# The first layer's input projection by seven products for eight

## The chip, the cores and the metric

One Trainium2 chip, of which the kernel uses one core. The metric is the device time of one execution in microseconds, as the median of the runs shown. A change of some 2% can be told from no change.

## The reference, cut to what matters

Two layers work on 512 latent and 256 context tokens of 2048 features. Each layer norms and modulates its input, projects it with `w_in` to three kinds of heads (HGRN2, mLSTM, attention), and projects the heads' outputs back with `w_out`.

```python
for layer in range(DEPTH):                       # 2
    mod_lat = (silu(c) @ w_mod[layer] + b_mod[layer])[:, None, :]
    mod_ctx = (silu(c_ctx) @ w_mod[layer] + b_mod[layer])[None, None, :]
    shift_l, scale_l, gate_l = jnp.split(mod_lat, 3, axis=-1)
    ...
    pl = split_proj(modulate(x, g_pre[layer], shift_l, scale_l) @ w_in[layer])
    pc = split_proj(modulate(h_ctx, g_pre[layer], shift_c, scale_c) @ w_in[layer])
    a_c, a_l = hgrn2_branch(pc, pl, ...)         # 4 heads
    b_c, b_l = mlstm_branch(pc, pl, ...)         # 4 heads
    c_c, c_l = attention_branch(pc, pl, ...)     # 8 query heads, 2 key heads
    y_lat = jnp.concatenate([a_l, b_l, c_l], axis=-1) @ w_out[layer]
    x = x + gate_l * rms_norm(y_lat, g_post[layer])
    ...
```

`modulate` is `rms_norm(h, gain) * (1 + scale) + shift`.

## The kernel before, in words

Features stand on the partitions, 16 tiles (`kt`) of 128; tokens stand in the columns. Every operand of the projection is a high and a low part in fp32r (`xs[o][kt]`, o = 0 the 512 latent columns, o = 1 two shift columns and the 256 context columns), and so is every weight: `load_w` (L303) loads a quarter of a feature tile's weights (256 KB, `raw`), copies the high part on ScalarE (L309) and subtracts it on VectorE (L310). A product then is three matmuls, high by high, high by low and low by high (L347). One output feature tile of the projection (`Proj`, `run_proj` L366) takes four quarters of four `kt`, each 3 x (512 + 258) columns. There are 61 such tiles in a layer: 20 for attention (`cq`, `ck`, `cv`, `cz`), one for the mLSTM's gates (`bg`, two matmuls for three), 20 for HGRN2 (`aq`, `af`, `ab`, `ai`, `ag`) and 20 for mLSTM (`bq`, `bk`, `bv`, `bo`, `bz`).

The norm's factor of each token (`rb`) is not part of the operand: it multiplies the finished product when VectorE takes it out of PSUM (`evac_`, L586). The shift goes through the projection in two columns of its own and is added as a bias behind it.

The order of the first layer: `emit_start` (L411) computes the modulation's scale on PE (`emit_mod`, L202) while it splits the rows and already multiplies the first six tiles (`EARLY`), whose shift follows by products of its own (L514). The modulation's shift comes by `emit_mods` (L232), and its gate by the same function beside the heads. Then `unit_c` (eight attention heads), `b_gates`, four times `unit_a` and four times `unit_b` run; each head calls `proj` for each of its tiles just before it needs it. `add_mod` (L248) meanwhile sums the next layer's shift and scale on VectorE, one row of weights at a time (L255, L257). The heads' results go to memory (`mixd`), one of them directly into an operand (`DIRECT`, L396), and `project_mid` (L1139) multiplies them with `w_out`. The second layer then does the same with its own weights.

A scheduler orders each engine's instructions ahead of time; what stands in a `high_priority` context goes first. Every DMA is issued from SP's queue in order. The heads' tiles have mostly one buffer each (`U`, `PAIR`), `raw`, `hi` and `lo` four, the staging tiles `st` seven. PSUM has eight banks: `psP` two times two, `psW` two, `psS` two.

## Time and profile before

| | us |
|---|---|
| median of 2 runs | 2874.87 (2874.21 to 2875.53) |
| span of the profiled execution | 2873.6 |
| PE busy | 2846.9 |
| PE weight loads busy | 2515.7 |
| DVE busy | 1867.5 |
| ACT busy | 1134.7 |
| POOL busy | 17.1 |

The span goes from the first to the last instruction of one profiled execution; the runs' times include what lies around it. PE is TensorE, DVE VectorE, ACT ScalarE, POOL GpSimd, SP the engine whose queue issues the DMAs. Matmul records overlap, so the pace of PE is read from how many matmuls a stretch holds and not from the mean of one record.

### The profile page before, as it was taken

The numbers are of one execution on the slowest core, as the hardware profiler recorded it, in microseconds if no ns is written. First come the engines' busy times: TensorE is split into PE (matmuls) and PEld (weight loads), VectorE is DVE, ScalarE is ACT, GpSimd is POOL, SyncE is SP. The second block draws the span as 40 slices with busy tenths as digits, with TensorE's granted clock in tenths as the row PEclk, the third lists the DMA queues.
The fourth block names the chain that finished last, engine by engine and source line by source line (L and its number), as shares of the span: only waits on it lengthen the run. The fifth ranks groups of instructions, "written<-read, shape, count | busy, mean of one in ns | idle before, by whom it ended". The sixth has DMA issues, their size and how long they took to land.

```text
span 2873.6 us, 51559 instructions
## 1 busy us (share of the span) xinstructions
PE 2846.9 (99%) x19849; PEld 2515.7 (88%) x19849; DVE 1867.5 (65%) x4203; ACT 1134.7 (39%) x2475; POOL 17.1 (1%) x32
## 2 busy tenths in 40 slices
PE   9999999999999999999999999999999999999998
PEld 4648878988888888888999999999899999999886
DVE  3405547667657868688768879567667665757526
ACT  3203423344433432332656654444533333333433
POOL 0000000000000000000000000000000000000000
PEclk9999999999999999999999999999999999999999
DMA  9564355322222325353667765224222222424545
GB/s 333 173 194 140 107 173 160 92 87 56 58 61 71 99 86 151 107 157 114 199 195 214 231 178 169 63 79 132 74 67 64 67 70 81 139 82 138 158 128 158
DMA packets 208280, 366.76 MB, mean 128 GB/s; under 512 B 24704, under 2 KB 42384, under 8 KB 207904
## 3 DMA queue, kind: packets, MB, share of 16 engines
q1 hardware_dynamic: 208032, 363.45, 42.1%
q8 instruction: 156, 2.56, 0.4%
q14 instruction: 92, 0.75, 0.1%
HBM read 345.08 MB, written 18.28 MB: 126 GB/s over the span
## 4 chain that ended last, share of the span: by engine, by line
PE 95%; ACT 2%; DVE 1%; DMA 1%; issue 1%; SPq 0%; DVEq 0%; ACTq 0%
PE pp L347 72%; PE pp L1329 6%; PE ops L1075 2%; PE modps L232 2%; PE scps L1035 2%; PE lv L788 2%; PE ptps L1068 1%; PE modps L202 1%; PE aops L869 1%; PE modp L263 1%; PE tps L626 1%; PE sps L851 1%; PE nps L962 1%; PE cps L942 1%; PE nps L960 1%
## 5 line engine op out<-in xcount | busy, mean ns | idle before, releaser
L347 PE MATMUL pp<-x0h,hi 128*128 128x256 f32 (+2 forms) x3088 | 942.1, 335 | 3.8 <-ACT x0h L398 2.3
L347 PE MATMUL pp<-x0l,hi 128*128 128x256 f32 (+2 forms) x3088 | 934.4, 332 | 0.0
L347 PE MATMUL pp<-x0h,lo 128*128 128x256 f32 (+1 forms) x3056 | 921.3, 332 | 0.0
L309 ACT CAST hi<-raw 128x512 fp32r<-128x512 f32 x764 | 472.3, 620 | 1084.3 <-PE pp L347 828.9
L310 DVE TENSOR_TENSOR lo<-raw,hi 128x512 fp32r<-128x512 f32 x764 | 526.2, 691 | 429.9 <-ACT hi L309 393.0
L347 PEld LDWEIGHTS pp<-x0h,hi 128*128 128x128 f32 x3088 | 544.6, 189 | 77.6 <-issue 15.3
L347 PEld LDWEIGHTS pp<-x0l,hi 128*128 128x128 f32 x3088 | 543.4, 189 | 66.7 <-issue 12.8
L347 PEld LDWEIGHTS pp<-x0h,lo 128*128 128x128 f32 x3056 | 536.5, 188 | 61.1 <-issue 9.2
L347 PE MATMUL pp<-x1h,hi 128*128 128x258 f32 (+1 forms) x1632 | 463.6, 285 | 0.3 <-ACT hi L309 0.3
L347 PE MATMUL pp<-x1l,hi 128*128 128x258 f32 (+1 forms) x1632 | 463.8, 284 | 0.0
L347 PE MATMUL pp<-x1h,lo 128*128 128x258 f32 (+1 forms) x1600 | 454.0, 284 | 0.4 <-DVE lo L310 0.2
L347 PEld LDWEIGHTS pp<-x1h,hi 128*128 128x128 f32 x1632 | 310.7, 190 | 14.0 <-issue 11.9
L347 PEld LDWEIGHTS pp<-x1l,hi 128*128 128x128 f32 x1632 | 308.6, 189 | 7.2 <-issue 6.9
L347 PEld LDWEIGHTS pp<-x1h,lo 128*128 128x128 f32 x1600 | 302.9, 189 | 5.6 <-issue 4.4
L257 DVE SCALAR_TENSOR_TENSOR scs<-st,sc,scs 128x512 f32<-128x512 f32 x180 | 135.4, 752 | 1.5 <-DMA st<-in_wmod 1.4
L257 DVE SCALAR_TENSOR_TENSOR mo<-st,sc,mo 128x512 f32<-128x512 f32 x180 | 135.4, 752 | 0.0
L1329 PE MATMUL pp<-lo,x0h 128*128 128x512 f32 x256 | 101.5, 396 | 0.0
L1329 PE MATMUL pp<-hi,x0h 128*128 128x512 f32 x256 | 101.3, 396 | 0.0
L1329 PE MATMUL pp<-hi,x0l 128*128 128x512 f32 x256 | 100.4, 394 | 0.0
L802 ACT COPY lvc<-aqq 128x256 f32<-128x256 f32 x140 | 60.4, 431 | 95.8 <-DVE aqq L810 74.7
L1069 ACT COPY pt<-ptps 128x512 f32<-128x512 f32 x96 | 47.5, 516 | 113.5 <-PE ptps L1068 113.0
L807 DVE TENSOR_TENSOR akk<-akk,aff 128x256 f32<-128x256 f32 x168 | 76.2, 453 | 9.3 <-PE ktps L835 7.0
(383 smaller groups left out, 3092.8 us busy)
## 6 DMA issues: line engine op xcount, KB each, us to landing
raw<-in_win SPq DMA_DIRECT2D x500, 256.0 KB, 2.7
st<-in_wmod SPq DMA_DIRECT2D x325, 256.0 KB, 2.9
raw<-in_wout SPq DMA_DIRECT2D x192, 256.0 KB, 3.2
raw<-in_wlast SPq DMA_DIRECT2D x80, 256.0 KB, 2.8
mw<-in_wmod SPq DMA_DIRECT2D x57, 256.0 KB, 5.3
st<-in_win SPq DMA_DIRECT2D x24, 256.0 KB, 3.9
xr<-in_xin SPq DMA_DIRECT2D x48, 128.0 KB, 3.5
st<-mixd SPq DMA_DIRECT2D x45, 128.0 KB, 3.6
```

Source lines behind the costliest of these rows:

```text
L232: prev = T.matmul(ps[32 * j:32 * j + 32, :], scs[:, 32 * kt:32 * kt + 32], ws[j], start=(i == 0 and (side or g == 0)), stop=(i == 1 and (s ...
L257: V.scalar_tensor_tensor(out=acc, in0=w, scalar=c, in1=acc, op0=ALU.mult, op1=ALU.add)
L309: S.copy(out=hi, in_=raw)
L310: lo_ins[:] = [V.tensor_tensor(out=lo, in0=raw, in1=hi.bitcast(F32), op=ALU.subtract).ins]
L347: T.matmul(dst, self.w[w][:, kt % 4, :], xs[o][kt][j][:, x0:x0 + n], start=(first and i == 0 and (self.outs is None or self.outs[k][1])), ...
L788: prev = T.matmul(lv[64 * c:64 * c + 64, o:o + 64], km[:, t0:t0 + 64], qm[:, t1:t1 + 64], start=True, stop=True, tile_position=(0, 64 * c) ...
L802: S.copy(out=mixed(qm.unsqueeze(1), 0, 256, b, 0), in_=mixed(Q2, c0, 256, b))
L807: V.tensor_tensor(out=x, in0=x, in1=blocks(F2, c0, b, b, 776, True), op=ALU.mult)
L1035: T.matmul(x[:, d0:d0 + len_], q[:, a, COLP[c]:COLP[c] + P], kr[:, b, k0:k0 + len_], start=(i == 0), stop=(i == 2))
L1069: S.copy(out=pt[:, 0:len(g) * P], in_=tp)
L1075: T.matmul(o[:, i * P:i * P + P], vt[kb], pt, start=(k == 0), stop=(k == len(mine) - 1))
L1329: x = T.matmul(ps[c], xs[0][kt][a][:, c * P:c * P + P], w[b].rearrange("p a b -> p (a b)"), start=(kt == kts[0] and i == 0), stop=(kt == k ...
```

## The change: what it does

The first layer's projection is no longer done tile by tile. The rows (2048 input features) are taken in two halves of eight `kt`. Within a half, a pair of output tiles (two 128-wide feature tiles), two groups of four `kt` and two halves of the tokens (256 latent, 2 shift and 128 context columns each, `BW` = 386) make a 2 x 2 by 2 x 2 block product. It is done with seven products for eight, with sums of blocks of the weights (`s1` to `s4`, on GpSimd) and of the rows (`T1`, `T2`, `T3`, `N4`, made once for each half). Accumulators in four PSUM banks (W, X, Y, Z) are copied out between products (`snap`) and added up (`end`). `bg` has no partner and takes four products of two matmuls.

The first half is done for all 31 units (`PAIRS`) in `emit_start`, before any head; partial sums go to memory (`pd`). The second half (`emit_second`) is done in the heads' phase, a pair when one of its tiles is first asked for; it loads the partial sums, adds to them (snapshots on GpSimd, ends on VectorE) and stores the finished products to memory (`qd`). A head then loads its product with three DMAs (`fetch`), and GpSimd multiplies it by `rb`.

The early tiles and their shift products are gone. Four chunks of the modulation come first (scale 4, 5 and shift 0, 1, of the first half's features); twelve others, the gate and the next layer's shift among them, are multiplied on PE beside the first half's products, and the next layer's scale is summed on VectorE there, so that none of it is left beside the heads. In the first layer there are four staging buffers, six for `raw` and three for `hi` and `lo`. The operands of `project_mid` and the second layer get their place after the first layer's heads.

```diff
+CSEQ = [n for g in range(2) for n in [f"ck{g}", f"cv{g}"] + [f"{p}{h}" for h in range(4 * g, 4 * g + 4) for p in ("cq", "cz")]]
+ASEQ = [f"{p}{h}" for h in range(4) for p in ("aq", "af", "ab", "ai", "ag")]
+BSEQ = [f"{p}{h}" for h in range(4) for p in ("bq", "bk", "bv", "bo", "bz")]
+PAIRS = [tuple(q[i:i + 2]) for q in (CSEQ, ["bg"], ASEQ, BSEQ) for i in range(0, len(q), 2)]
...
+    class Pool:
+        st, raw, hl, stp = 4, 6, 3, None
+        def tile(self, *a, **k):
+            return self.pool.tile(*a, **k)
+    wp, psP = Pool(), Pool()
...
+    pd, qd = ({n: tc.dram_tile([P, 2, BW], F32, name=f"{c}_{n}") for u in PAIRS for n in u} for c in ("pd", "qd"))
...
+    def emit_mod(l, n):
         ps = sps(512, "modps")
-        for kt in range(KT):
-            if kt == 8 and between is not None:
-                between()
-            if kt < len(slots):
-                w = slots[kt]()
-                nc.sync.dma_start(w, I["wmod"][l, n, kt])
-            else:
-                w = stage(I["wmod"][l, n, kt])
-            j = kt % 4
-            T.matmul(ps[32 * j:32 * j + 32, :], scs[:, 32 * kt:32 * kt + 32], w,
-                     start=(kt < 4), stop=(kt >= 12), tile_position=(0, 32 * j))
+        for g in range(4):
+            ws = [stage(I["wmod"][l, n, 4 * g + j]) for j in range(4)]
+            prev = None
+            for j in (3, 2, 1, 0):
+                kt = 4 * g + j
+                with tc.issue_after(prev) if prev is not None else nullcontext():
+                    prev = T.matmul(ps[32 * j:32 * j + 32, :], scs[:, 32 * kt:32 * kt + 32], ws[j],
+                                    start=(g == 0), stop=(g == 3), tile_position=(0, 32 * j)).ins
+            if g < 3:
+                yield
...
+    B11, B21, T2, T1, T3, B22, N4 = [(g, i) for g in range(4) for i in range(2)][0:7]
+    XB = {}
...
+    def squares(sc, b, first):
+        if first:
+            acc[0] = sc.tile([P, 2, BW], F32, name="acc")
+            S.activation(out=acc[0], in_=b, func=AF.Square)
+        else:
+            sq = sc.tile([P, 2, BW], F32, tag="sq", name="sq")
+            S.activation(out=sq, in_=b, func=AF.Square)
+            G.tensor_tensor(out=acc[0], in0=acc[0], in1=sq, op=ALU.add)
...
+    def sum_blocks(sc, j, b1, b2, E):
+        t1, t2 = (sc.tile([P, BW], F32, tag=f"t{i}{j}", name=f"t{i}{j}") for i in range(2))
+        E.tensor_tensor(out=t1, in0=b1[:, 1], in1=b1[:, 0], op=ALU.subtract)
+        E.tensor_tensor(out=t2, in0=b2[:, 1], in1=t1, op=ALU.subtract)
+        E.tensor_tensor(out=b1[:, 1], in0=b2[:, 1], in1=b1[:, 1], op=ALU.subtract)
+        return t1, t2
...
+    def split_blocks(bs, E):
+        for blk in (B11, B21, T2, T1, T3, B22, N4):
+            g, i = blk
+            for j, (b1, b2, t1, t2) in enumerate(bs):
+                src = {B11: b1[:, 0], B21: b2[:, 0], T2: t2, T1: t1, T3: b1[:, 1], B22: b2[:, 1], N4: t2}[blk]
+                if blk == N4:
+                    E.tensor_tensor(out=t2, in0=b2[:, 0], in1=t2, op=ALU.subtract)
+                if i == 0:
+                    XB[g, j] = [wp.tile([P, 2 - (g == 3), BW], F32R, tag=f"X{g}{j}{c}", name=f"X{g}{c}") for c in "hl"]
+                h, lo = (x[:, i] for x in XB[g, j])
+                S.copy(out=h, in_=src)
+                V.tensor_tensor(out=lo, in0=src, in1=h.bitcast(F32), op=ALU.subtract)
...
+    def split_w(src):
+        hi, lo = (wp.tile([P, 4, P], F32R, tag=c, name=c, bufs=wp.hl) for c in ("hi", "lo"))
+        S.copy(out=hi, in_=src)
+        V.tensor_tensor(out=lo, in0=src, in1=hi.bitcast(F32), op=ALU.subtract)
+        return hi, lo
...
+    def add_w(a, b, op, tag=None):
+        o = wp.tile([P, 4, P], F32, tag=tag, name=tag, bufs=1) if tag else b
+        G.tensor_tensor(out=o, in0=a, in1=b, op=op)
+        return o
+    def product(ps, w, blk, first, parts=((0, 0), (0, 1), (1, 0))):
+        g, i = blk
+        for j in range(4):
+            for k, (a, b) in enumerate(parts):
+                T.matmul(ps[:, 0:BW], w[a][:, j, :], XB[g, j][b][:, i], start=(first and j == 0 and k == 0),
+                         stop=(j == 3 and k == len(parts) - 1), skip_group_check=not first)
...
+    def two_tiles(l, unit, half, psx, snap, end):
+        bank = lambda t: psx.tile([P, 512], F32, tag=t, name=f"ps{t}")
+        src = lambda f, k: raw_w(I["win"][l, TIDX[unit[f]], 2 * half + k])
...
+        with urgent():
+            a11, a12, a21, a22 = src(0, 0), src(0, 1), src(1, 0), src(1, 1)
+            w = split_w(a11)
+        X = bank("X")
+        product(X, w, B11, True)
+        snap(0, 0, X)
+        with urgent():
+            w = split_w(a12)
+            s1 = add_w(a21, a22, ALU.add, "s1")
+            s2 = add_w(s1, a11, ALU.subtract, "s2")
+        W = bank("W")
+        product(W, w, B21, True)
+        end(0, 0, W)
+        with urgent():
+            w = split_w(s2)
+        product(X, w, T2, False)
+        snap(0, 1, X)
+        with urgent():
+            w = split_w(s1)
+            s3 = add_w(a11, a21, ALU.subtract)
+        Y = bank("Y")
+        product(Y, w, T1, True)
+        snap(1, 1, Y)
+        with urgent():
+            w = split_w(s3)
+            s4 = add_w(a12, s2, ALU.subtract)
+        product(X, w, T3, False)
+        snap(1, 0, X)
+        end(1, 1, X)
+        with urgent():
+            w = split_w(s4)
+        product(Y, w, B22, False)
+        end(0, 1, Y)
+        with urgent():
+            w = split_w(a22)
+        Z = bank("Z")
+        product(Z, w, N4, True)
+        end(1, 0, Z)
...
+        g = emit_mod(0, 4)
+        next(g)
+        early_consts()
+        list(g)
+        list(emit_mod(0, 5))
+        bs = []
+        for j in range(4):
+            b = raw_blocks(sc, j, j)
+            for i, x in enumerate(b):
+                squares(sc, x, i == j == 0)
+                scale_blocks(0, x, j + 4 * i)
+            bs.append((*b, *sum_blocks(sc, j, *b, V)))
+        split_blocks(bs, V)
+        for n in (0, 1):
+            list(emit_mod(0, n))
+        put_shifts(sc)
+        late_consts()
...
+        adds = [(1, 4 + j, kt) for j in range(4) for kt in range(KT)]
+        for u, unit in enumerate(PAIRS):
+            pt = [wp.tile([P, 2, BW], F32, tag="pt", name="pt", bufs=3) for _ in unit]
+            def snap(f, h, ps, sign=1):
+                with tc.high_priority():
+                    S.activation(out=pt[f][:, h], in_=ps[:, 0:BW], func=AF.Copy, scale=float(sign))
+            def end(f, h, ps, n=len(unit)):
+                with tc.high_priority():
+                    if n == 1 and h == 0:
+                        S.copy(out=pt[f][:, h], in_=ps[:, 0:BW])
+                    else:
+                        V.tensor_tensor(out=pt[f][:, h], in0=ps[:, 0:BW], in1=pt[f][:, h], op=ALU.add)
+                    if (f, h) in ((0, 1), (1, 0)):
+                        nc.sync.dma_start(pd[unit[f]], pt[f])
+            two_tiles(0, unit, 0, psx, snap, end)
+            prio[0] = True
+            for _ in range(2):
+                mod_step()
+            for _ in range(2 + u % 2):
+                if adds:
+                    add_mod(*adds.pop(0), accs=accs)
+            if u >= 21 and u - 21 < 4:
+                j = u - 21
+                if j == 0:
+                    bs = []
+                b = raw_blocks(sc, j, 8 + j)
+                for i, x in enumerate(b):
+                    kt = 8 + j + 4 * i
+                    squares(sc, x, False)
+                    scale_blocks(0, x, kt)
+                    G.tensor_copy(x[:, 0, 256:258], modt[0][:, kt, :])
+                bs.append((*b, *sum_blocks(sc, j, *b, G)))
+        while adds:
+            add_mod(*adds.pop(0), accs=accs)
+        split_blocks(bs, G)
+        cols = [acc[0][:, h, c:c + P] for h in range(2) for c in (0, P)] + [acc[0][:, h, 258:BW] for h in range(2)]
+        token_rstd(const, cols, 6, rb, (0, CO), "rs")
...
+    def emit_second(psx):
+        def second_half(unit):
+            pt = []
+            with urgent():
+                for nm in unit:
+                    pt.append(wp.tile([P, 2, BW], F32, tag="pt", name="pt", bufs=3))
+                    nc.sync.dma_start(pt[-1], pd[nm])
+            def snap(f, h, ps, sign=1):
+                with tc.high_priority():
+                    t = wp.tile([P, BW], F32, tag="sn", name="sn", bufs=4)
+                    S.activation(out=t, in_=ps[:, 0:BW], func=AF.Copy, scale=float(sign))
+                    G.tensor_tensor(out=pt[f][:, h], in0=pt[f][:, h], in1=t, op=ALU.add)
+            def end(f, h, ps):
+                with tc.high_priority():
+                    V.tensor_tensor(out=pt[f][:, h], in0=ps[:, 0:BW], in1=pt[f][:, h], op=ALU.add)
+                    if (f, h) in ((0, 1), (1, 0)):
+                        nc.sync.dma_start(qd[unit[f]], pt[f])
+            two_tiles(0, unit, 1, psx, snap, end)
+            made.update(unit)
+        return second_half
...
+                while nm not in made:
+                    second_half(units.pop(0))
...
+        def fetch(nm, dst):
+            nc.sync.dma_start(dst[:, 0:NL].rearrange("p (h c) -> p h c", h=2), qd[nm][:, :, 0:256])
+            nc.sync.dma_start(dst[:, NL:NL + 130], qd[nm][:, 0, 256:BW])
+            nc.sync.dma_start(dst[:, NL + 130:XW], qd[nm][:, 1, 258:BW])
...
+                fetch(nm, dst)
+                G.tensor_tensor(out=dst[:, 0:XW], in0=dst[:, 0:XW], in1=rb, op=ALU.mult)
...
+    units, made = list(PAIRS), set()
+    with tc.tile_pool(name="ws", bufs=1) as ws, \
+            tc.tile_pool(name="psX", bufs=1, space=bass.MemoryType.PSUM) as psx:
+        wp.pool = ws
+        with tc.tile_pool(name="first", bufs=1) as sc:
+            wp.stp = sc
+            emit_start(sc, psx)
+        second_half = emit_second(psx)
+        emit_lb()
+        with tc.tile_pool(name="unit0", bufs=1, reuse_waits="tile") as up:
+            run_units(0, False, up, [])
+    wp.st, wp.raw, wp.hl, wp.stp = 7, 4, 4, None
+    xp = ctx.enter_context(tc.tile_pool(name="xp", bufs=1, reuse_waits="tile"))
+    for kt in range(KT):
+        if kt != DIRECT:
+            new_x(kt, xp)
+    wp.pool = ctx.enter_context(tc.tile_pool(name="wp", bufs=1, reuse_waits="tile"))
+    psP.pool = ctx.enter_context(tc.tile_pool(name="psP", bufs=2, space=bass.MemoryType.PSUM, reuse_waits="tile"))
+    with tc.tile_pool(name="post0", bufs=1, reuse_waits="tile") as pp:
```

## Rows read from the trace of the kernel before

**Rows 1.** The page, part 1: engine, busy us (share of the span), instructions.
```profile
PE 2846.9 (99%) x19849; PEld 2515.7 (88%) x19849; DVE 1867.5 (65%) x4203; ACT 1134.7 (39%) x2475; POOL 17.1 (1%) x32
```

**Rows 2.** Stretches: us, busy of PE, PEld, DVE, ACT, POOL (instructions), clock, DMA share, GB/s.
```profile
0.00:230.00 230.00, 222.48 (x1019) 119.66 (x1020) 68.25 (x170) 49.98 (x84) 0.20 (x4) 0.99 0.69 229
230.00:626.00 396.00, 394.99 (x2621) 340.48 (x2620) 240.45 (x497) 144.20 (x288) 1.48 (x2) 1.00 0.42 129
626.00:1020.00 394.00, 392.14 (x2929) 343.96 (x2929) 277.04 (x680) 163.78 (x413) 0.21 (x1) 1.00 0.24 68
726.26:826.51 100.25, 100.25 (x750) 88.13 (x750) 64.07 (x162) 39.35 (x102) 0.00 (x0) 1.00 0.21 57
1020.00:1419.00 399.00, 399.00 (x2548) 360.11 (x2547) 308.63 (x657) 140.25 (x334) 8.62 (x15) 1.00 0.45 131
```

**Rows 3.** The chain of waits: start, us, what.
```profile
925.89 30.91 PE pp L347 x176
...
1500.05 83.40 PE pp L347 x708
...
2692.28 36.62 PE pp L1329 x158
```

**Rows 4.** PE, 230 to 1419 us, groups by shape: count | busy us, mean ns.
```profile
L347 PE MATMUL pp<-x0h,hi 128*128 128x512 f32 x874 | 349.4, 400 | 0.3 <-DVE aqq L586 0.3
...
L1075 PE MATMUL ops<-pt,lvc 128*128 128x128 f32 x352 | 44.3, 275 | 0.0
L1035 PE MATMUL scps<-ckr,cqr 128*128 128x256 f32 x192 | 28.6, 286 | 0.0
...
L1068 PE MATMUL ptps<-c_ident,pr 128*128 128x128 f32 x176 | 25.8, 274 | 0.0
...
L232 PE MATMUL modps<-st,scs 128*32 128x512 f32 x128 | 17.0, 605 | 0.0
```

**Rows 5.** DVE, 230 to 1419 us, groups by line.
```profile
L310 DVE TENSOR_TENSOR lo<-raw,hi 128x512 fp32r<-128x512 f32 x231 | 159.8, 692 | 124.8 <-ACT hi L309 117.9 <-PE tps L626 4.5 <-DMA raw<-in_win 1.5
L257 DVE SCALAR_TENSOR_TENSOR scs<-st,sc,scs 128x512 f32<-128x512 f32 x120 | 90.4, 753 | 1.5 <-DMA st<-in_wmod 1.4
...
L807 DVE TENSOR_TENSOR akk<-akk,aff 128x256 f32<-128x256 f32 x84 | 38.3, 456 | 1.6 <-ACT aff L756 0.3
...
L586 DVE TENSOR_TENSOR zb<-pp,rb 128x770 f32<-128x770 f32 x8 | 7.7, 965 | 1.3 <-PE lv L788 1.3
```

**Rows 6.** POOL in order of time: start us, us, instruction, idle before.
```profile
1157.61 0.86 POOL L918 TENSOR_SCALAR_AFFINE_SELECT dexp<-dexp 128x768 f32<-128x768 f32 x1 [43.98 <-DVE mo L257]
...
1345.59 0.86 POOL L918 TENSOR_SCALAR_AFFINE_SELECT dexp<-dexp 128x768 f32<-128x768 f32 x1 [43.75 <-DVE scs L257]
1347.86 1.13 POOL L918 TENSOR_SCALAR_AFFINE_SELECT dexp<-dexp 128x768 f32<-128x768 f32 x1 [1.41 <-ACT dexp L915]
...
2486.13 0.63 POOL L918 TENSOR_SCALAR_AFFINE_SELECT dexp<-dexp 128x512 f32<-128x512 f32 x1 [72.26 <-ACT dexp L915]
```

**Rows 7.** DVE in order of time, at two of those moments.
```profile
1158.03 0.98 DVE L310 TENSOR_TENSOR lo<-raw,hi 128x512 fp32r<-128x512 f32 x1 [0.50 <-ACT hi L309]
...
1345.38 0.96 DVE L586 TENSOR_TENSOR zv<-pp,rb 128x770 f32<-128x770 f32 x1
```

**Rows 8.** DMA: loads, KB, us to landing; and the first 72 us.
```profile
st<-in_wmod SPq DMA_DIRECT2D x325, 256.0 KB, 2.9
...
DMA packets 13828, 23.96 MB, mean 333 GB/s; under 512 B 2816, under 2 KB 3200, under 8 KB 13824
```

**Rows 9.** All engines in order of time, at the start and at the heads' end.
```profile
19.82 1.05 PE L207 MATMUL modp<-c_sel,mo 128*128 128x2 f32 x8 [0.79 <-DVE mo L204]
...
217.53 0.69 DVE L238 COPY mo<-modps 128x512 f32<-128x512 f32 x1 [7.26 <-PE modps L232]
...
221.43 0.39 PE L347 MATMUL pp<-x1h,hi 128*128 128x258 f32 x1
...
1404.66 0.69 DVE L396 TENSOR_TENSOR x0l<-mix,x0h 128x512 fp32r<-128x512 f32 x1
```

More of the change, by code (lines that the diff above doesn't have):

```diff
@@ L22 @@
 XW = NL + 2 + NC
+BW = 386
 CO = NL + 2
@@ new lines, in emit, with scale_blocks @@
+    acc = [None]
+    def squares(sc, b, first):
[6 more added lines that the diff above has]
+            G.tensor_tensor(out=acc[0], in0=acc[0], in1=sq, op=ALU.add)
+    def scale_blocks(l, b, kt):
+        for v, c in enumerate((slice(0, 256), slice(258, BW))):
+            S.activation(out=b[:, :, c], in_=b[:, :, c], func=AF.Copy, scale=gs[l][:, kt, v:v + 1])
```

330 lines of the change are left out of this document (134 added, 196 removed).

## Prediction

> **What bounds the kernel now.** I read the page's busy shares first [rows 1]: TensorE (PE) is busy 99% of the span and VectorE (DVE) 65%. That PE share alone proves little, because matmul records overlap, so I went to the chain of waits [rows 3]: long runs of matmuls with nothing between them. 176 projection matmuls, alternately 512 and 258 columns wide, take 30.91 us: 351 ns per pair. 708 of 256 columns take 83.40 us (117.8 ns each), 158 of 512 columns 36.62 us (231.8 ns). PE is paced by columns and is the bound from about 23 us on. The table of stretches [rows 2] then says what stands next to it: between 230 and 1419 us DVE works 240.45 + 277.04 + 308.63 = 826 us of 1189, so it has 30% left; GpSimd (POOL) does almost nothing. One HGRN2 head takes 100.25 us: five tiles of 16 x 3 x 0.351 = 16.85 us make 84.2, so 16.0 us are the head's own PE work, and DVE is busy 64.07 us beside it. The first layer's heads end when the last mixed head is split, at 1406 us [rows 9]. What follows is the same code before and after but for pools, 2873.6 - 1406 = 1467 us.
>
> **The change, part by part.** The sum is made against the profiled span; the median of the runs lies 1.3 us above it, which I add at the end.
>
> *Products.* 386 columns lie between two measured widths: 117.8 + 130 x (231.8 - 117.8)/256 = 175.7 ns. One of the seven products of half a pair has 4 x 3 matmuls, 2.11 us; a pair's half takes 7 x 2.11 = 14.75 us, against 2 x 16.85 / 2 = 16.85 before. Thirty pairs, both halves: 60 x (16.85 - 14.75) = 126 us less for PE. The gates' tile has no partner and costs the same 11.2 us as before.
>
> *Start.* Before, the first product runs at 23 us, while the modulation still arrives, and the first 230 us hold only six tiles (101 us of products). After, nothing is multiplied until four chunks of the modulation (scale 4 and 5, shift 0 and 1) are in, since a product needs scaled, summed and split rows with their shift columns. Loads run through four staging buffers, and the four matmuls of a group are queued behind the load issued last. So a group costs its landing, 2.9 us for one load, about 0.7 us for each of three more (256 KB at the 333 GB/s of the first 72 us would be 0.79) [rows 8], and 1.06 us of matmuls (17.0 us for 16 groups [rows 4]): 6.0 us. 16 groups: 96 us. Add 4 us to the first load and the last chunk's way to the first product, 3.9 us from copy to matmul [rows 9], with the shift columns 6: first product at 106 us. Bounds: 85 if transfers overlap better, 125 if landings are as slow as when everything loads at once. The splitting of the rows lies under those loads.
>
> *First half of the rows.* 30 x 14.75 + 5.6 = 448 us of products. Twelve further chunks of modulation stand on PE beside them: 48 x 1.06 + 12 x 1.05 for their sums over partitions [rows 9] = 64 us; four chunks on DVE end in matmuls, 6 us. Together 518 us. Per pair (17.3 us of PE) DVE has seven splits, four additions and 2.5 modulation rows of two 0.75 us operations: 4.8 + 2.2 + 3.8 = 10.8 us, so PE stays the bound. The staging ring is tight: 10.5 loads per pair through four buffers of some 6 us a turn are 15.8 us. If it were slower, up to 25 us.
>
> *Between the halves.* The second half's split rows take the tiles of the first. Their order is that of the products, and a block's split (4 x 0.55 us) is as long as a product, so little shows: 8 us, from 3 to 20.
>
> *Second half with the heads.* Products 448 us. The heads' own PE work: in 1177 us up to 1406, 858 full steps (of 874) of 3 x 0.351 us and 16 of the gates are 915 us, output projection 12, gates' modulation 17, sums 15; 218 remain. PE alone would need 448 + 218 = 666 us, where before the same heads were spread over some 1180. This is the point on which the change hangs: DVE's work for the heads is not reduced by as much. Its groups in that stretch [rows 5] (some 120, four of the largest shown) add up to 921 us; 160 are weight splits, 188 modulation, 53 the scaling by the norm, 24 other, and 496 the heads. Records overlap a little (826 busy of 921 added, 0.90), so the heads are 445 us. Each pair adds 7 x 0.62 us of splits and 4 x 0.50 us of additions out of PSUM, 6.3 us. The scaling goes to POOL.
>
> I take this half in two. Attention: PE has ten pairs, 98.7 us of head work in three groups [rows 4] and some 16 in smaller ones, 262 us; DVE has 124 of the heads (138 added, of lines 1007 to 1077 and of the queries' and gates' lines 589 and 600) and 63 of the pairs, 187. PE binds, 262. The rest: PE has 404 us; DVE has 445 - 124 = 321 and 20.5 x 6.3 = 129, 450 us. **DVE binds there**, and with no gap at all.
>
> POOL is the disputed cost. Per pair it gets four additions of 512 columns, four of 386, and two scalings of 770. No row shows a two-input operation on POOL; the nearest are one-input masks, 0.63 us for 512 columns and 0.86 for 768 [rows 6]. By those (low end) a pair costs 4 x 0.63 + 4 x 0.53 + 2 x 0.86 = 6.4 us; if its inputs are read one after the other (high end) 12.8. In the rest that is 130 to 260 us. The rows show that it isn't free to DVE: a split that takes 0.69 us took 0.98 [rows 7] when it began 0.42 us into a mask of 0.86, as long as if it had waited for the mask's end, and a mask begun under a DVE operation took 1.13 instead of 0.86. About three quarters of DVE's time is in operations that read SBUF twice or copy it, like these; those out of PSUM were not lengthened (0.96 us for a scaling [rows 7] with the mask of 1345.59 us beside it, as on average [rows 5]). [...]
>
> I take the low price, nearest in size and engine, and half of it as delay (65 us), since POOL also runs under DVE's PSUM operations and under the heads' waits for PE and ScalarE. Second half: 262 + 450 + 65 = 777 us.
>
> Moving the products through memory costs no engine time of its own. The fetches stand in SP's queue, where one that waits for its tile holds the weight loads behind it; six raw buffers cover about a pair and a half of products, so I price it at nothing, 20 us if that cover is gone. The early shift products (some 8 us on PE) fall away in the start. DMA volume grows by about 60 tiles x four passes of 0.39 MB, 95 MB, at about 43% busy engines in this stretch [rows 2]: hidden.
>
> **The sum.** 106 + 518 + 8 + 777 + 1467 = 2876, and 1.3: 2877 us. The gain of the seventh product is given back because the heads no longer have their products' time to hide DVE in.
>
> **The rivals.**
> (a) PE stays the bound, or DVE without delay: products run ahead and POOL's work falls in gaps. T of the second half 666 to 712, total 2766 to 2812. For it: the order of each engine is free to mix pairs into the heads' waits, and DVE's average use in the second half, (445 + 190)/712, would still be under 90%. Against it: after attention DVE's own work already exceeds PE's.
> [...]
> (c) The change doesn't do what it says: PE stalls inside the first half, on the staging ring or on snapshots that must leave a bank before the next product adds to it. A bank has one product (2.1 us) of grace against about 0.5 us on ScalarE. Ring and start at their upper bounds: 2877 + 19 + 25 = 2921.
>
> **How the numbers follow.** Forecast (2815 to 2932) with (c) 0.44, (a) 0.27, (b) 0.29. Forecast's own range 2815 to 2930. To hold 8 in 10 the range takes in most of both sides: 2775 to 2980. Within 2% (2817 to 2932), about what a measurement can tell from no change, 0.44; faster by more 0.27, slower by more 0.29.
>
> **What would show it.** First product near 106 us; first half about 518 us with matmuls 176 ns apart; then, after attention, DVE above 85% busy and PE with idle stretches that DVE or POOL end. [...] I am wrong if the first half isn't bound by PE, if POOL's two-input price lies outside 0.63 to 1.27 us, or if the mixed heads end well before the products do.

## The result, and the profile after

The changed kernel takes 3214.3 us (3213.6 to 3215.0), against 2874.9 us before: ratio 1.118, 95% interval 1.115 to 1.122. The forecast was 2877 us (2775 to 2980). The kernel is 339 us slower, and no case I had worked out reaches so far.

The first two parts of the page of the changed kernel, to be set beside [rows 1]:

```profile
PE 2792.9 (87%) x19065; PEld 2568.5 (80%) x19065; DVE 2221.5 (69%) x4474; ACT 1360.6 (42%) x2953; POOL 679.1 (21%) x495
...
PE   2599999987899888873337999999999999999998
...
PEclk9999999999999999986668999999999999999999
```

The rows of digits show the span in 40 slices, the busy share of each in tenths. PE, which filled 99% of the span, now has two holes: the first two slices, and three slices of 3 from 1445 us on (18 slices of 80.3 us), in which its granted clock falls too. The table of stretches of the changed kernel shows the same by stage (us, then busy time of PE, PEld, DVE, ACT and POOL, the granted clock, the DMA share and GB/s); its counterpart is [rows 2].

```profile
0.00:138.00 138.00, 40.43 (x169) 10.82 (x169) 39.94 (x111) 38.51 (x68) 32.64 (x24) 1.00 0.59 195
138.00:704.00 566.00, 541.76 (x3126) 484.19 (x3126) 364.30 (x552) 200.19 (x385) 193.34 (x144) 0.99 0.67 216
704.00:1065.00 361.00, 322.08 (x1970) 309.07 (x1971) 292.98 (x474) 182.72 (x379) 200.81 (x140) 0.96 0.45 143
1065.00:1420.00 355.00, 298.35 (x1968) 277.67 (x1966) 325.34 (x544) 169.46 (x393) 186.12 (x136) 0.95 0.40 128
1420.00:1720.00 300.00, 117.50 (x870) 102.36 (x870) 201.17 (x542) 108.97 (x315) 59.33 (x41) 0.68 0.19 58
1720.00:3211.00 1491.00, 1472.77 (x10965) 1384.37 (x10965) 997.79 (x2255) 660.77 (x1417) 6.85 (x10) 0.99 0.42 130
```

Read from the top: 138 us until the first product; 566 us of the first half of the rows, PE almost full; attention beside the second half's products until 1065; HGRN2 heads beside products until 1420, DVE 92% busy; then 300 us in which the heads are alone, PE 39% and DVE 67% busy, so that no engine is full; then the same end as before. DVE's timeline of the changed kernel shows when each mixed head leaves (HGRN2 heads `ag`, mLSTM heads `bz`; two of the latter left out); before, the last left at 1403 us and was split at 1406 [rows 9]:

```profile
1229.46 0.68 DVE L778 TENSOR_TENSOR mix<-mixps,ag 128x512 f32<-128x512 f32 x1
...
1363.47 0.68 DVE L778 TENSOR_TENSOR mix<-mixps,ag 128x512 f32<-128x512 f32 x1
...
1466.12 0.69 DVE L778 TENSOR_TENSOR mix<-mixps,ag 128x512 f32<-128x512 f32 x1 [1.70 <-PE mixps L776]
...
1541.72 0.68 DVE L778 TENSOR_TENSOR mix<-mixps,ag 128x512 f32<-128x512 f32 x1
...
1588.96 0.69 DVE L778 TENSOR_TENSOR mix<-mixps,bz 128x512 f32<-128x512 f32 x1 [1.63 <-PE mixps L776]
...
1717.38 0.69 DVE L778 TENSOR_TENSOR mix<-mixps,bz 128x512 f32<-128x512 f32 x1 [1.63 <-PE mixps L776]
```

While products run beside it, an HGRN2 head takes 134 us (1229 to 1363). Alone it takes 75 us (1466 to 1542), and an mLSTM head alone some 45. The last product is stored at 1426 us, when two HGRN2 heads and all four mLSTM heads are still to be finished: the products have run ahead of the heads.

DVE's groups of the changed kernel, 704 to 1720 us (busy us, mean ns, idle time before); splits were 692 ns before [rows 5]:

```profile
L466 DVE TENSOR_TENSOR lo<-raw,hi 128x512 fp32r<-128x512 f32 x119 | 106.8, 898 | 14.7 <-ACT hi L465 14.5
L466 DVE TENSOR_TENSOR lo<-s,hi 128x512 fp32r<-128x512 f32 x90 | 74.7, 834 | 5.9 <-ACT hi L465 5.5
L961 DVE TENSOR_TENSOR aqq<-aqq,aff 128x256 f32<-128x256 f32 x84 | 59.9, 713 | 0.9 <-ACT lvc L953 0.6 <-DVE lvc L952 0.3
L958 DVE TENSOR_TENSOR akk<-akk,aff 128x256 f32<-128x256 f32 x84 | 52.6, 626 | 1.1 <-ACT aff L907 0.6
...
L952 DVE COPY lvc<-akk 128x256 f32<-128x256 f32 x84 | 35.2, 419 | 0.1
```

POOL's additions by line (ns: least, median, most), all of two inputs: weight sums of 512 columns (one of the four kinds left out), and the second half's additions of 386:

```profile
L480 POOL TENSOR_TENSOR raw<-raw x62: 1263/1413/1899, 33.5 to 1393.7; 128x512 f32<-128x512 f32 x62
L480 POOL TENSOR_TENSOR s<-s,raw x60: 1259/1464/2545, 32.3 to 1395.7; 128x512 f32<-128x512 f32 x60
L480 POOL TENSOR_TENSOR s<-raw,s x60: 1264/1295/2866, 35.4 to 1409.0; 128x512 f32<-128x512 f32 x60
...
L647 POOL TENSOR_TENSOR pt<-pt,sn x121: 858/1068/5412, 704.1 to 1418.6; 128x386 f32<-128x386 f32 x121
```

The least weight sum, 1.26 us, is my high bound for POOL, and the medians (1.29 to 1.46) lie beyond it; I had taken the low one, 0.63, from masks [rows 6].

### The profile page after: what moved, and what is told of

Same layout as the page of the kernel before. It is cut to its first block, busy times and chain, and to the rows that moved or that the text cites. A ratio compares the mean times of both kernels' runs of the same rounds, so it can differ in the third digit from the quotient of the medians.

```text
span 3211.4 us, 52468 instructions
## 1 busy us (share of the span) xinstructions
PE 2792.9 (87%) x19065; PEld 2568.5 (80%) x19065; DVE 2221.5 (69%) x4474; ACT 1360.6 (42%) x2953; POOL 679.1 (21%) x495
## 4 chain that ended last, share of the span: by engine, by line
PE 50%; DVE 9%; issue 3%; DMA 3%; ACT 2%; POOL 1%; SPq 0%; DVEq 0%; POOLq 0%; ACTq 0%
PE pp L324 32%; PE pp L1474 5%; PE psX L487 2%; PE ops L1226 1%; PE lv L939 1%; PE psY L487 1%; DVE lo L466 1%; PE scps L1186 1%; PE psW L487 1%; DVE akk L958 1%; DMA st<-mixd 1%; PE ptps L1219 1%; DVE aqq L961 1%; PE nps L1111 1%; DVE aff L962 1%
## 5 line engine op out<-in xcount | busy, mean ns | idle before, releaser
L324 PE MATMUL pp<-x0h,hi 128*128 128x256 f32 (+1 forms) x2112 | 551.6, 304 | 1.2 <-ACT hi L286 1.1
L324 PE MATMUL pp<-x0l,hi 128*128 128x256 f32 (+1 forms) x2112 | 547.2, 302 | 0.0
L324 PE MATMUL pp<-x0h,lo 128*128 128x256 f32 (+2 forms) x2096 | 540.5, 302 | 0.1
L324 PEld LDWEIGHTS pp<-x0h,hi 128*128 128x128 f32 x2112 | 361.1, 189 | 16.0 <-ACT hi L286 1.6
L324 PEld LDWEIGHTS pp<-x0l,hi 128*128 128x128 f32 x2112 | 361.0, 189 | 15.7
L324 PEld LDWEIGHTS pp<-x0h,lo 128*128 128x128 f32 x2096 | 356.3, 189 | 13.8 <-DVE lo L287 0.5
L324 PE MATMUL pp<-x1h,hi 128*128 128x258 f32 (+1 forms) x656 | 186.6, 285 | 4.7 <-ACT x1h L373 4.1
L324 PE MATMUL pp<-x1l,hi 128*128 128x258 f32 (+1 forms) x656 | 187.5, 286 | 0.3 <-DVE x1l L374 0.3
L324 PE MATMUL pp<-x1h,lo 128*128 128x258 f32 (+1 forms) x640 | 182.2, 286 | 0.8 <-DVE lo L287 0.7
L480 POOL TENSOR_TENSOR s<-raw,s 128x512 f32<-128x512 f32 x60 | 88.0, 1466 | 343.2 <-DVE lo L466 297.6
L324 PEld LDWEIGHTS pp<-x1h,hi 128*128 128x128 f32 x656 | 126.2, 193 | 6.0 <-ACT x1h L373 4.5
```

The lines of the kernel that those rows point to most:

```text
L324: T.matmul(dst, self.w[w][:, kt % 4, :], xs[o][kt][j][:, x0:x0 + n], start=(first and i == 0 and (self.outs is None or self.outs[k][1])), ...
L480: G.tensor_tensor(out=o, in0=a, in1=b, op=op)
```

## The experiments

In what follows "the heads' stretch" is from the end of the first half (703 us, the same in most runs) to the split of the last mixed head; it was 1016 us in the changed kernel. A time without an interval is a single run's, read beside the changed kernel's 3214.3; the runs of one kernel lie up to 13 us apart (3192.9 to 3206.0), so single differences of 5 or 10 us say nothing by themselves.

**Products first.** The edit:

```
+            while units:
+                second_half(units.pop(0))
+            with tc.issue_after(last_end[0]):
+                fetch_(nm, dst)
```

> The computation is whole; only the order changes: no head of the first layer fetches a finished product before the last product of the second half has left its bank. So the second half falls into products alone (P) and heads alone (H), and the time is about 704 + P + H + 1491 us (the stretches before and behind are those of the changed kernel). Theory 'late heads' (the heads are a serial chain that now starts only at 704 us, and the products no longer cover it): P near 455 us (30 pairs of 14.75 us and the gates), since nothing but PE binds products that stand alone, and H 600 to 680 us (four HGRN2 heads of 75 us and four mLSTM heads of 47 us, as the changed kernel's last ones take when alone, and about 130 for attention); total 3250 to 3330. Rival 'POOL's price' (sums of weights and of products on POOL at 1.2 to 1.5 us pace the products themselves): P above 560 us, over 18.5 us per pair, and total above 3350 or H well under 600.

Measured: 3310.5 us. The tie of SP's fetches to DVE's last addition held nothing back: POOL scales the first fetched product at 733 us, and attention went on beside the products. What the run did is to put all products ahead of all heads in the program's order. The last product was stored at 1314 us for 1426, and the last head ended at 1818 for 1719, with HGRN2 heads of 73 us and mLSTM heads of 46, all eight alone. P and H can't be read apart, so the numbers fit by the total only. What follows: products that end 112 us earlier gave nothing; heads that came later ended 99 us later.

**Heads first.**

```
+            prio[0] = False
             two_tiles(0, unit, 1, psx, snap, end)
+            prio[0] = True
```

> The loads, sums and splits of the second half's weights lose their precedence over the heads' instructions; all else is as in the changed kernel. Theory 'late heads' with products that run ahead: products then spread over the heads, the stretch in which heads run alone with PE at 40% (1426 to 1720 us) shrinks, and the time falls to 2950 to 3100 us. [...]

Measured: 3224.4 us, ratio 1.120 (1.119 to 1.122): not the 2950 to 3100 of my theory. The heads' last split is at 1734 us, and again the products are all stored (1436 us) long before. The loads' precedence isn't why products run ahead: the order of the engines lets them run ahead with or without it.

**No POOL.**

```
-                    S.activation(out=t, in_=ps[:, 0:BW], func=AF.Copy, scale=float(sign))
-                    G.tensor_tensor(out=pt[f][:, h], in0=pt[f][:, h], in1=t, op=ALU.add)
+                    V.tensor_tensor(out=pt[f][:, h], in0=pt[f][:, h], in1=ps[:, 0:BW],
+                                    op=ALU.add if sign > 0 else ALU.subtract)
...
-                G.tensor_tensor(out=dst[:, 0:XW], in0=dst[:, 0:XW], in1=rb, op=ALU.mult)
+                V.tensor_tensor(out=dst[:, 0:XW], in0=dst[:, 0:XW], in1=rb, op=ALU.mult)
...
-        G.tensor_tensor(out=o, in0=a, in1=b, op=op)
+        (G if prio2[0] else V).tensor_tensor(out=o, in0=a, in1=b, op=op)
```

> In the second half nothing of the products or of the scaling is left on POOL: the sums of weights and the scaling by the norm run on DVE, and the partial sums are added by DVE straight out of PSUM, without the copy on ScalarE. [...] Theory 'late heads': DVE gets some 6 us more per pair of products (190 us in a stretch of 1016 in which it is busy 830), wins some 80 back by shorter splits, and the time stays between 3170 and 3290, with the heads still alone at the end.

Measured: 3204.4 us, ratio 1.113 (1.110 to 1.115). The stretch from 704 to 1710 us in this run (columns as above), and DVE's groups in it:

```profile
704.00:1710.00 1006.00, 725.90 (x4798) 690.30 (x4796) 802.40 (x1850) 413.92 (x959) 10.48 (x18) 0.86 0.36 113
```

```profile
L467 DVE TENSOR_TENSOR lo<-raw,hi 128x512 fp32r<-128x512 f32 x118 | 81.0, 686 | 1.8 <-ACT hi L466 1.5
...
L648 DVE TENSOR_TENSOR pt<-pt,psX 128x386 f32<-128x386 f32 x91 | 50.3, 553 | 12.3 <-PE psX L488 12.1
L960 DVE TENSOR_TENSOR akk<-akk,aff 128x256 f32<-128x256 f32 x84 | 37.8, 449 | 3.4 <-ACT aff L909 3.1
L963 DVE TENSOR_TENSOR aqq<-aqq,aff 128x256 f32<-128x256 f32 x84 | 37.6, 448 | 1.2 <-ACT lvc L955 1.2
L954 DVE COPY lvc<-akk 128x256 f32<-128x256 f32 x84 | 24.6, 292 | 0.1
...
L481 DVE TENSOR_TENSOR s<-raw,s 128x512 f32<-128x512 f32 x30 | 20.7, 689 | 0.3
```

The decays (the multiplications that write `aqq` and `akk`) took 713 and 626 ns beside POOL and take 448 without it; copies 419 and 292, splits 898 and 686. A weight sum costs DVE 0.69 us, POOL 1.26 or more. DVE is busy 802 us here and was busy 819 in the changed kernel (293, 325 and 201 in the table of stretches), though it now also does 118 weight sums (81 us), 121 more additions (67 us) and all scalings. So what POOL took off DVE came back as longer DVE operations, and a little more. Copies, which read one source, are drawn out as well as decays and splits, which read two; why POOL's work lengthens them no run shows. Yet the kernel gains 10 us only, hardly more than the runs differ among themselves, and stays where the theory had it (3170 to 3290): the products are stored by 1315 us, 111 earlier than in the changed kernel, but the first HGRN2 head leaves at 1295 for 1229, so that more of the heads stand alone; none is faster alone, and they end at 1710. POOL's price is real, but moving its work to DVE doesn't win it back.

**Six staging buffers.** `st` is 6 for 4 before the second half.

> Six staging buffers for four until the second half begins (eight don't fit in the memory), so that a group of modulation weights can be half under way while the one before it is multiplied. Theory (a group waits for its own landing, 7.4 us per group before the first product): first product between 110 and 128 us instead of 138, time 3185 to 3205. Rival (the transfers themselves set the pace): first product above 132 us and the time within 6 us of 3214.

Measured: 3195.2 us, ratio 1.111 (1.109 to 1.113). PE's timeline in the start, first of the changed kernel, then of this run:

```profile
113.60 1.93 PE L214 MATMUL modps<-st,scs 128*32 128x512 f32 x8 [5.74 <-DMA st<-in_wmod]
120.98 1.94 PE L214 MATMUL modps<-st,scs 128*32 128x512 f32 x8 [5.44 <-DMA st<-in_wmod]
...
137.87 0.69 PE L487 MATMUL psX<-X0h,hi 128*128 128x386 f32 x1
```

```profile
95.76 1.93 PE L214 MATMUL modps<-st,scs 128*32 128x512 f32 x8 [3.46 <-DMA st<-in_wmod]
101.15 1.93 PE L214 MATMUL modps<-st,scs 128*32 128x512 f32 x8 [3.45 <-DMA st<-in_wmod]
...
108.68 0.69 PE L487 MATMUL psX<-X0h,hi 128*128 128x386 f32 x1
```

A group's turn falls from 7.4 to 5.4 us and the first product from 137.9 to 108.7, as the theory had it (expected were 110 to 128); 19 of the 29 us reach the end.

**No products in the second half.**

```
         def second_half(unit):
+            made.update(unit)
+            return
```

> Left out: all products of the second half with their loads, sums and splits; the heads fetch the first half's partial sums. What stands between the end of the first half (703 us) and the last head's end is then the heads alone (H). Theory 'late heads' (a serial chain of some 640 us: four HGRN2 heads of 75 us, four mLSTM heads of 47, attention and gates about 150): H between 600 and 680 us and a time of 2790 to 2880 us, so that with 450 us of PE's work gone the kernel only just equals the one before. Rival 'the products hold the heads up by precedence' with a short chain: H under 550 us and a time below 2740.

Measured: 2911.9 us, 302 less than the changed kernel and still 37 more than the kernel before. The heads take 717 us (703 to 1420), with HGRN2 heads of 73 us and mLSTM heads of 46. I had expected 600 to 680 and a time of 2790 to 2880; attention and gates are longer, some 240 us for 150. This is the main finding: with 450 us of PE's work taken out, the kernel is no faster than the old one, because the heads' chain begins at 703 us and is 717 us long. Before, the same heads stood under the products from 230 us on. DVE is busy 491 of these 717 us (704 to 1420, first two rows in the section on matmuls alone): for 225 us it waits for the heads' own matmuls, ScalarE, POOL and fetches.

**No low halves and sums; few matmuls.** Two runs with one part of the products each left out (`first_half[0]` is false in the second half):

```
+        if not first_half[0]:
+            return hi, hi
...
+        if not first_half[0]:
+            return a
```

> Left out in the second half: the low halves of the weights on DVE and the sums of weights on POOL; every product uses the high half twice, so PE, ScalarE, the loads and the additions of partial sums are as before. Theory 'DVE's own work is what each pair adds to the heads' chain' (splits of 0.83 to 0.90 us, and heads' operations drawn out by POOL's sums): 209 splits of 0.87 us, 181 us, and part of the lengthening go, time 2960 to 3050. Rival 'PE's products stand in the heads' way' (in-order queue, 2.1 us a product): time above 3120.

Measured: 3080.7 us, 134 less; the heads' stretch 884 us. More than I had put for this theory's end, less than the rival's.

```
+        js = range(4) if first_half[0] else range(1)
+        for j in js:
```

> Left out in the second half: three in four matmuls of each product; all loads, sums, splits and additions stay. Rival 'PE's products stand in the heads' way': 336 us of PE go and the time falls below 2990. Theory 'DVE's own work': the time stays above 3080, since DVE and POOL have all their work.

Measured: 3209.0 us, 5 less, which a single run doesn't tell from nothing. By itself this says that matmuls cost nothing; the run of matmuls alone, below, refutes it. Here too the products run ahead (stored by 1265 us), and the first HGRN2 head leaves late, at 1311 us.

**No copies and additions.** The second half's `snap` does nothing, and `end` adds only the last of a tile's two blocks.

> Left out in the second half: ScalarE's copies of a product and POOL's additions of them to the partial sums (121), and half of DVE's additions out of PSUM; one in two remains, which lets the result be stored. All matmuls, weight loads, sums and splits of weights stay. Of the 300 us by which the products lengthen the heads' stretch (1017 us with them, 716 without), leaving out low halves and weight sums took 134 back, and leaving out three in four matmuls 5. Theory 'each pair adds its DVE, POOL and ScalarE work to the heads' chain': this takes 60 to 150 us back, time 3065 to 3155. Rival (only the splits do harm, since only they are on the way to a product): time above 3190.

Measured: 3149.7 us, 65 less.

**Matmuls alone.**

```
+            for t, blk, first in (("X", B11, True), ("W", B21, True), ("X", T2, False), ("Y", T1, True),
+                                  ("X", T3, False), ("Y", B22, False), ("Z", N4, True)):
+                product(bank[t], fix, blk, first)
```

> Of the second half's products only the matmuls are left, all seven of each pair, on one weight tile that is split once: no loads, splits, sums or additions, and the heads fetch the first half's partial sums, as in the run without products (2912 us, heads' stretch 716 us at a granted clock of 0.64 to 0.70). It tells whether the run with a quarter of the matmuls (3209 us) hid a price of the matmuls behind a lower clock. Theory (PE's products cost the heads nothing): time 2850 to 2925, less than 2912 where the clock is higher. Rival (2.1 us of product ahead of a head's matmul is a price): time above 2950.

Measured: 3025.9 us, 114 more than without products: my theory that PE's products cost the heads nothing falls. Stretches of the run without products, of that with few matmuls and of that with matmuls alone, in this order (columns as above):

```profile
704.00:1065.00 361.00, 170.58 (x1271) 149.74 (x1272) 254.80 (x575) 160.64 (x374) 56.28 (x32) 0.69 0.15 43
1065.00:1420.00 355.00, 139.47 (x999) 121.47 (x997) 236.69 (x601) 128.97 (x375) 67.00 (x46) 0.64 0.19 54
```

```profile
704.00:1065.00 361.00, 227.69 (x1002) 181.90 (x1000) 335.65 (x470) 179.68 (x372) 246.41 (x173) 0.72 0.53 168
1065.00:1420.00 355.00, 176.39 (x1097) 136.26 (x1097) 302.47 (x589) 168.48 (x398) 144.51 (x102) 0.66 0.34 103
```

```profile
704.00:1065.00 361.00, 348.46 (x2354) 341.60 (x2353) 207.48 (x445) 139.25 (x305) 48.62 (x27) 0.98 0.14 40
1065.00:1420.00 355.00, 298.65 (x2211) 288.13 (x2209) 222.73 (x575) 114.63 (x330) 54.83 (x35) 0.92 0.14 41
```

With matmuls alone PE is 97% busy in the first stretch, DVE only 57%, and a head's matmul stands behind products: HGRN2 heads of 84 to 89 us for 73, though the granted clock is higher. With few matmuls DVE is 93% busy there, so the heads may wait for it instead; the clock is at 0.72 and 0.66, so what matmuls gave back may in part be lost by slower ones. The two runs show neither reason by itself.

**Both omissions together.**

> Both omissions together: in the second half no low halves, no weight sums, no copies and additions of partial sums but one per bank pair for the store. Left are loads, ScalarE's high halves and all matmuls. If the two prices add (134 and 65 us, each measured alone), the time is 2995 to 3035; if they were one and the same wait, it stays above 3045; if together they give more than the sum, it falls below 2985. What then still stands above the run without products (2912) is the loads', the high halves' and the order's.

Measured: 3054.2 us, 160 less than the changed kernel and 142 more than without products. The two prices, 134 and 65, make 199 and not 160: they overlap. Against the 142 that are left stand 114 for matmuls alone; since prices overlap, that is no share of them.

**Landing tiles for the heads alone.** To the run without products (the fetch also gets precedence, and `raw` has five buffers for six):

```
+                with tc.high_priority():
+                    ld = wp.tile([P, 776], F32, tag="ld", name="ld", bufs=3)
+                    fetch(nm, ld)
+                G.tensor_tensor(out=dst[:, 0:XW], in0=ld[:, 0:XW], in1=rb, op=ALU.mult)
```

> The heads alone again (the second half's products left out, the heads fetch the first half's partial sums), but each fetch lands in one of three tiles of its own, ahead of its use, and POOL scales it from there into the head's tile; the heads' other work is as it was. To be compared with the run without products, where the heads took 716 us (703 to 1419) and the kernel 2912. Theory 'the trip through memory stands on the heads' chain' (there the fetches of an mLSTM head and SP's issue of them made some 13 of its 46 us, those of an HGRN2 head 2 of 73): mLSTM heads of 36 to 40 us, time 2850 to 2885. Rival (the fetches are hidden, as I had priced them): time within 10 us of 2912.

Measured: 2891.2 us, 21 less than without landing tiles, outside both. In the changed kernel's chain of waits an mLSTM head has such pieces:

```profile
1591.68 2.60 DMA bz<-qd_bz
...
1600.00 3.69 DMA zb<-qd_bk
...
1603.86 1.82 POOL zb L717
...
1622.89 2.42 DMA zb<-qd_bq
```

But with the fetches landed ahead, mLSTM heads still take 45 to 50 us, the last excepted: the chain passes over to the next step, and my 36 to 40 falls. The gain lies before the first HGRN2 head leaves (12 us) and in the other three (3 to 4 us each). So the trip through memory is exposed to the heads, at some 20 us by these two single runs. That this is also the figure that I had named for lost cover is chance: mine was for weight loads held up behind a fetch, and here there are none.

> As the run with landing tiles for the heads alone, but DVE scales the fetched product instead of POOL, so that nothing of the heads but masks and zeros is left on POOL. Theory (POOL's scaling of 1.3 to 2.0 us stands on the chain and draws DVE's operations out): 15 to 45 us less than that run. Rival (DVE is the heads' bound, and work moved to it is added to the chain): 10 to 40 us more.

Measured: 2885.6 us, 6 less than that, below the 15 that I had put for the theory, and as near to nothing as single runs can tell.

**Mended.** The edits of the runs with six buffers and without POOL, and two landing tiles.

> The whole computation, with what the runs pointed to: six staging buffers before the second half, all of POOL's weight sums, additions and scalings of the second half on DVE (partial sums straight out of PSUM), and two landing tiles, so that fetches run ahead of the heads. Theory 'late heads': the start gives 19 us, the fetches 30 to 60, POOL's part 10 to 20, time 3100 to 3160, still over 7% slower than the kernel before, because the heads' own chain of about 700 us begins only after the first half. If it came below 2950, the lateness of the heads would not be the cause.

Measured: 3164.1 us, ratio 1.101 (1.099 to 1.103), 4 us above what I expected and far from 2950. The 50 us gained are the 19, 10 and 21 that the three edits gave one by one; for the fetches I had put 30 to 60.

**Eight products over the same halves.**

```
+        for f in range(len(unit)):
+            ps = [bank(t) for t in ("WX", "YZ")[f]]
+            for k, blks in enumerate(((B11, B12), (B21, B22))):
+                with urgent():
+                    w = (split_gates if two else split_w)(src(f, k))
+                for h in range(2):
+                    product(ps[h], w, blks[h], k == 0, **two)
+            for h in ((0, 1), (1, 0))[f]:
+                end(f, h, ps[h])
```

> The whole computation, with the two halves of the rows, the partial sums through memory and the heads' fetches as in the changed kernel, but eight plain products for seven: no sums of weights or rows, four splits per pair and half for seven, no snapshots; sums stay in the banks. Theory (PE isn't what binds the second half; DVE, POOL and ScalarE work per pair is): the first half gets 63 us longer (30 products of 2.11 us), the second half shorter by 110 to 160 us (DVE per pair 4 x 0.69 + 4 x 0.55 = 5.0 us for 8.5, no POOL), time 3115 to 3170. Rival (PE's products bind both halves): 63 us more in each, time above 3300.

Measured: 3119.4 us, ratio 1.086 (1.084 to 1.088): 95 us faster than seven. The stretches of the first half, with eight products:

```profile
138.00:740.00 602.00, 600.68 (x3500) 548.77 (x3501) 188.86 (x331) 143.55 (x280) 1.55 (x8) 0.99 0.65 206
```

PE has a gap of 1 us here, where with seven it had 24 us in 566. The last partial sum of the first half leaves its bank at 735 us for 703: of the 63 us that seven products for eight should save PE in the first half, 32 reach the clock on the wall. In the second half eight products leave the heads a stretch of 888 us (735 to 1623) for 1016. So of the 339 us lost, 245 stand with the halves, the late start of products and heads and the trip through memory, and 95 with the scheme of sums itself.

## Why the prediction was wrong, step by step

*Products*: right. Twelve matmuls take 2.13 us in the chain of waits of the changed kernel, 178 ns each for my 175.7:

```profile
1204.10 2.13 PE psX L487 x12
```

*Start*: 138 us for 106, above my bound of 125. A group took 7.4 us in the rows shown, and 8.1 on the mean of all sixteen, for 6.0: its matmuls 1.94 for 1.06, which makes 14 of the 32 us, and its wait 5.4 to 5.7 in those rows. The run with six buffers shows the mechanism right; the landing and the matmuls were mis-sized.

*First half*: 566 us for 518. PE was busy 542, so 24 us are idle (11 of them before modulation matmuls that wait for their loads, some 12 before the halves of a split weight, by PE's groups) and the rest is matmul time that I counted too low. That the idle time comes near rival (c)'s 25 us is chance: (c) put them down to the ring, and the ring's waits make 11.

*Between the halves* is inside these stretches: PE is busy 48 of 60 us from 700 to 760, 12 us for my 8.

*Second half with the heads* is the step that failed: 1016 us for 777. I had put it together as attention bound by PE (262), DVE "with no gap at all" (450) and half of POOL's low price (65), which is 637 us of DVE work, 75 of idle DVE in attention, and 65. Measured are 819 us of busy DVE (for 637 and 65) and 197 idle (for 75), so both terms fell short, by some 120 us each.
- The busy term: POOL's true price is at least twice the low bound (1.26 us and more for 0.63), and beside it DVE's operations are longer by as much as it relieves DVE (819 us busy with POOL, 802 without; decays 713 and 626 ns for 448). The 65 us of the sum, half of the low price, were my estimate of that delay. But the same run shows that it isn't the way out: with the work on DVE the time is the same within 0.3%.
- The idle term: I let the products fill the heads' waits. A single head's operations wait for one another on PE, ScalarE, POOL and memory, and DVE idles 225 us when the heads are alone. Products could fill that only if they lasted as long as the heads. They run ahead, are out at 1426 us, and leave 300 us with DVE 67% busy. Neither less precedence nor more moved this to the better.

Behind it stands what I didn't price as a bound: the length of the heads' chain by itself, which is the heads one after another in the order and with the single buffers that this kernel gives them. It is 717 us with nothing beside it, and by cutting the products into halves the change lets it begin at 703 us instead of under the first products. 703 + 717 + 1490 is 2910 already. Rivals (a) and (c), like the forecast, had heads that are paced by an engine's sum of work; (a) would have needed 666 to 712 us, less than the chain alone. I named a danger ("if the mixed heads end well before the products do") with the wrong sign: the heads ended 293 us after the last product was stored.

*Fetches through memory*, priced at nothing: 21 us by the run with landing tiles for the heads alone, where the heads wait for the landing itself; my 20 us were for another wait, that of weight loads behind a fetch.

*The rest*: 1492 us for 1468 from the end of the last split on, 24 us longer; the same 1490 stand in the run without products. 21 of the 24 are lost by the end of the output projection's first pass, 94 us behind the split before and 115 after. I had counted the stretch from the heads' end as one that the change leaves alone. But before, the output projection began under the last head: 114 of its matmuls, 256 columns wide and worth 13 us, were done from 1389 us on. After, its operands get their place only behind the heads, and its first matmul comes 2 us after the split, at a granted clock of 0.61 (1719 to 1731 us). PE's timeline and the chain of waits, before and then after:

```profile
1389.31 0.29 PE L347 MATMUL pp<-x1h,hi 128*128 128x256 f32 x1
...
1499.60 0.44 PE rbps L164 x4
```

```profile
1721.47 0.80 PE L324 MATMUL pp<-x1h,hi 128*128 128x256 f32 x2 [4.13 <-ACT x1h L373]
...
1834.68 0.44 PE rbps L179 x4
```

That the place of the operands is the reason is read from the kernel and these rows; no run moved it.

*Readings*: two are off, without weight in the sum. A split beside a mask took 0.98 us, not "as long as if it had waited for the mask's end", which would be 0.44 and 0.69, 1.13 us. And the DMA engines' share over the stretch of the heads was 0.37, not 43%: the three rows say 0.42, 0.24 and 0.45.

What stays open besides: how the 302 us that the products cost the heads divide. Matmuls alone cost 114, splits with weight sums 134 when taken out, copies and additions 65; they overlap, and the clock changes along with them. It is open too how much of the 717 us is the clock's doing (the last section has an estimate), and no run gave the heads' tiles a second buffer, so that heads could overlap each other.

## What to carry to other kernels

Before work is moved to a later stage, take the time of the chain that must follow it, alone, with all its waits, and compare that with the work which is left to cover it; an engine's sum of work is only a lower bound. A saving on the bound engine is worth what it is where that engine is still the bound: here an eighth fewer products, with the sums that they need, saved 32 us in the first half and lost 128 in the second, beside the heads. Work put on POOL beside a busy DVE should be priced also at what it adds to DVE's operations: here as much as it took off DVE (819 us busy with POOL, 802 without).

## What the runs showed of the hardware

In the changed kernel an addition of two inputs of 512 columns on POOL took 1.26 us at the least and up to 2.9; 386 columns took 0.86 to 5.4 us. On DVE the same addition took 0.69 us in the run without POOL.

How a DVE operation lengthens beside POOL can be seen in the timelines of the changed kernel, DVE's first: a split that began 0.5 us into POOL's sum took 1.31 us for 0.68. That is 0.14 us less than if it had waited for the sum's end, 0.77 us later, and then run; the prediction's split beside a mask [rows 7] was short of that by 0.15.

```profile
1185.53 0.68 DVE L466 TENSOR_TENSOR lo<-s,hi 128x512 fp32r<-128x512 f32 x1
1186.81 1.31 DVE L466 TENSOR_TENSOR lo<-s,hi 128x512 fp32r<-128x512 f32 x1 [0.61 <-ACT hi L465]
```

```profile
1186.28 1.30 POOL L480 TENSOR_TENSOR s<-raw,s 128x512 f32<-128x512 f32 x1 [7.54 <-DVE lo L466]
```

The granted clock was 0.68 on average where PE was 39% busy (1420 to 1720 us), and 0.69 and 0.64 in the run without products; with matmuls beside the heads it was 0.98 and 0.92. The same small matmuls of an mLSTM head took 112 ns each in the chain of the kernel before, beside products at a granted clock of 1.00, and 215 in that of the changed kernel, with the heads alone:

```profile
1370.01 0.67 PE nps L962 x6
```

```profile
1561.75 1.29 PE nps L1113 x6
```

In the run without products PE's pieces make 142 of the 717 us of the heads' chain. Had all of them gone at the pace of 112 ns for 215, the chain would be some 70 us shorter; this is an estimate, and an upper one, as not all of them can have been slowed by as much. So leaving work out of that stage also changed the pace of what stayed, and the 717 us are the heads alone at that clock.

In the start the modulation's groups took 1.94 us for 1.06 while the row of that stretch shows a granted clock of 1.00 (PE had idled 3 to 8 us before each); beside the first half's products they took 1.07 (47 groups in 50.1 us of busy PE). The column doesn't account for it, and no run here does.
